# Query products as three fp32r products, the context modulated on GpSimd

## The chip, the cores and the metric

The kernel runs on one core of a Trainium2 chip. The metric is the device time of one execution in microseconds (us), lower is better. Before the change three runs took 1552.02, 1554.79 and 1555.33 us, a median of 1554.79 us.

The five engines of the core each work through their own queue in order: PE (TensorE, the matrix unit; its weight loads are listed as PEld), DVE (VectorE), ACT (ScalarE), POOL (GpSimd) and SP (SyncE, which here only issues DMAs). They wait for one another by semaphores.

## What is computed

The program runs two layers of a transformer with conditioning and a third block with a state-space branch and a mixture of experts, in float32, for 256 tokens and a width of 1024. The change touches only the beginning: the modulated RMS norm of the tokens `x` and of the context `ctx` (256 tokens each), and the query projection of the first attention. Cut to that:

```python
def rmsnorm(x, g):
    y = x * lax.rsqrt(jnp.mean(x * x, axis=-1, keepdims=True) + 1e-6)
    return y * g

def modulate(x, shift, scale):
    return x * (1.0 + scale) + shift

# layer 0: shift and scale are columns of silu(c) @ ada_w + ada_b
h  = modulate(rmsnorm(x,   norm1_g), shift,   scale)      # from c
hc = modulate(rmsnorm(ctx, norm1_g), shift_c, scale_c)    # from c_ctx
q, k, v = jnp.split(h @ wqkv, 3, axis=-1)
qc, kc, vc = jnp.split(hc @ wqkv, 3, axis=-1)
# only k and v are needed of the context
```

## The kernel before

Tokens lie along the free axis and the 1024 features along eight groups of 128 partitions, so `x[:, n]` and `cx[n]` are tiles of 128 by 256. The program is one long list of instructions per engine, in the order in which the Python code calls them; no scheduler moves anything.

**Precision.** Most products take three fast fp32r matmuls (`mm3`): a weight tile `w` is cut into a high part `wh` (ScalarE copy, line 146) and a low part `wl` (VectorE subtraction, line 134), the activations into `hH` and `hL`, and the product is wh·hH + wh·hL + wl·hH. `Stream.split_to(u)` cuts weight units up to u; a unit is 128 by 1024, eight 128 by 128 tiles. Weights come in megabyte DMAs (two units) through a ring of four buffers `st`.

**The query stage** is the loop `for n in ks` over the eight groups n of input features. It alone uses plain fp32 matmuls: `Stream.raw()` hands out the uncut weight unit of group n, and line 625 multiplies its eight tiles with `full`, the modulated `x` of group n. The sums of all eight output tiles stay in four PSUM buffers `ps_q` until the end of the loop.

Shift and scale of group n come up in the same loop. `products(n)` multiplies a megabyte of conditioning weights (line 512, in the middle of tile n-2), ScalarE copies the result to `pa_s` (line 515), `columns(n)` turns it into four columns of `raw` by small matmuls (line 523, at the end of tile n-2). `finish_x(n)` then makes shift and scale of `x` on VectorE (lines 492 and 493), `modulate` multiplies `x` by the scale and the row of reciprocal norms (`na`, line 529, VectorE), and ScalarE adds the shift twice, into `full` (line 532) and `hH` (line 533); VectorE makes `hL` (line 534). This is done for group n+1 after two of the eight products of group n.

**The context** needs the sums of its squares (`sums(cx)`, end of tile 0), its reciprocal norms (`row_rstd(1, ...)`, end of tile 2), and then the same modulation: `modulate_c` does up to two groups at the end of each tile from n = 3 on, with shift and scale on ScalarE (lines 498 and 499), the multiplication on VectorE and the split on both. GpSimd does nothing in this stage.

**The key stage** follows at once: eight tiles of 24 fp32r products each, which read `hH` and `hL` of `x` and the context side by side, 512 columns wide, so it needs all sixteen groups modulated, and weight unit 8 cut (`split_to(n + 3)` in the last two tiles).

Of the kernel before, what the change touches and what calls it, by code (L numbers as in the profile page):

```python
# [8 lines left out]
F32 = mybir.dt.float32  # L9
# [3 lines left out]
AF = mybir.ActivationFunctionType  # L13
ALU = mybir.AluOpType
# [3 lines left out]
P = 128  # L18
T = 256
D = 1024  # L20
KD = 8
# [86 lines left out]
class Stream:  # L108
# [51 lines left out]
    def more(self, n, defer=False):  # L160

        self.fill(self.pos // 8 // 2 + self.ring)
        self.split_to(self.pos // 8 + n, defer)

    def raw(self):

        u = self.pos // 8
        w = self.slots[u // 2][:, u % 2].rearrange("p (a c) -> p a c", a=8)
        if u % 2:
            del self.slots[u // 2]  # L170
        self.pos += 8
        self.nu = max(self.nu, u + 1)
        return w

    def take(self, n, ahead=None):

# [248 lines left out]
def build(ctx, tc, ap):  # L425
    b = Builder(ctx, tc, ap)
    nc = tc.nc
    ctx.enter_context(tc.manual_schedule())
    cp = ctx.enter_context(tc.tile_pool(name="const", bufs=1))
# [8 lines left out]
    x = cp.tile([P, KD, T], F32, name="x")  # L438
# [31 lines left out]
    ks = range(KD)  # L470
# [19 lines left out]
    def finish_x(n):  # L490

        nc.vector.tensor_scalar(AB[n][:, 0, 0:1], raw[:, n, 0:1], b.vecs[:, ab + n:ab + n + 1], None, op0=ALU.add)
        nc.vector.tensor_scalar(AB[n][:, 1, 0:1], raw[:, n, 2:3], b.vecs[:, n1 + n:n1 + n + 1], bsc[:, n:n + 1],
                                op0=ALU.mult, op1=ALU.add)

    def finish_c(n):

        nc.scalar.activation(AB[n][:, 0, 1:2], raw[:, n, 1:2], AF.Identity, bias=b.vecs[:, ab + n:ab + n + 1])
        nc.scalar.activation(AB[n][:, 1, 1:2], raw[:, n, 3:4], AF.Identity, bias=bsc[:, n:n + 1],
                             scale=b.vecs[:, n1 + n:n1 + n + 1])  # L500

    parts_ = {}

# [13 lines left out]
    def columns(n):  # L517

        if n >= KD:
            return  # L520
        p_ = parts_.pop(n)
        for j in range(2):
            nc.tensor.matmul(raw[:, n, 2 * j:2 * j + 2], lhsT=p_[:, j * P:(j + 1) * P], rhs=b.cst("sel"), start=False, stop=True,
                             skip_group_check=True)

    def modulate(src, rows, n, i, full=None):

        t = b.wk.tile([P, T], F32, tag="na", name="na", bufs=3)
        nc.vector.scalar_tensor_tensor(t, src[n], AB[n][:, 1, i:i + 1], rows, op0=ALU.mult, op1=ALU.mult)
        yield  # L530
        if full is not None:
            nc.scalar.activation(full, t, AF.Identity, bias=AB[n][:, 0, i:i + 1])
        nc.scalar.activation(hH[:, n, 1 - i], t, AF.Identity, bias=AB[n][:, 0, i:i + 1])
        nc.vector.scalar_tensor_tensor(hL[:, n, 1 - i], t, AB[n][:, 0, i:i + 1], hH[:, n, 1 - i], op0=ALU.add, op1=ALU.subtract)
        yield

    for n in ks:
        AB[n] = cp.tile([P, 2, 2], F32, name=f"ab{n}")
    nc.scalar.activation(bsc[:, :2], b.ones2, AF.Silu)
    st.limit = 0  # L540
    for i in range(2):
# [50 lines left out]
    columns(1)  # L592
    rows_x, rows_c = rps[:, :T], rps[:, T:]
    psq = [b.ps.tile([P, 2, T], F32, tag="ps", name="ps_q") for _ in range(4)]
    ready, fulls = [], {}

    def modulate_x(n):
        finish_x(n)
        fulls[n] = b.wk.tile([P, T], F32, tag="rp_b", name="full", bufs=2)
        for _ in modulate(xs, rows_x, n, 0, fulls[n]):  # L600
            pass

    def modulate_c():
        todo = []
        for i in ready[:2]:
            finish_c(i)
            todo.append(modulate(cx, rows_c, i, 1))
            next(todo[-1])
        del ready[:2]
        for o in todo:  # L610
            next(o)

    modulate_x(0)
    for n in ks:
        w = st.raw()
        for i in range(KD):
            if i == 2 and n + 1 < KD:
                modulate_x(n + 1)
            if i == 2 and n == 2:
                total(1, accs_c)  # L620
            if i == 5 and n == 2:
                r4 = rstd_of(1)
            if i == 4:
                products(n + 2)
            nc.tensor.matmul(psq[i // 2][:, i % 2], lhsT=w[:, i], rhs=fulls[n], start=(n == 0 and i % 2 == 0), stop=(n == KD - 1),
                             skip_group_check=True)
        columns(n + 2)
        if n == 0:
            accs_c = sums(cx)
        if n == 2:  # L630
            row_rstd(1, r4)
        ready.append(n)
        if n >= 3:
            modulate_c()
        if n in (1, 3, 4, 5, 6):
            load_w()
        if n == 3:
            nc.scalar.dma_start(crow[:, 0], ap["c"].to_broadcast([P, D]))
            nc.scalar.dma_start(crow[:, 1], ap["c_2"].to_broadcast([P, D]))
        if n == 4:  # L640
            for t_, o in ((b.csts, "csts"), (b.vecs, "vecs")):
                c0 = CHEAD if o == "csts" else VHEAD
                nc.scalar.dma_start(t_[:, c0:], ap[o][:, c0:])
        if n >= KD - 2:
            st.nu = max(st.nu, KD)
            st.split_to(n + 3)
    while ready:
        modulate_c()
    st.limit = st.n
    nc.scalar.activation(qT[:, 0:2], psq[0], AF.Copy, scale=0.125)  # L650
    st.more(2)
# [1662 lines left out]
```

## Time and profile before

| | |
|---|---|
| median of 3 runs | 1554.79 us |
| the profiled execution | 1555.31 us |
| its span in the profile | 1553.5 us |
| PE busy | 1483.4 us, 95% of the span |
| DVE, ACT, POOL busy | 986.0, 669.0 and 274.2 us |
| mean granted TensorE clock | 0.989 |

Times within the profile count from the start of the span. The query stage runs from 20.9 to 62.5 us, the key stage from 62.1 to about 107 us. A timeline row gives the start, the duration, the engine, the line and what is written from what; durations include the time an instruction takes to drain, so that neighbours of one engine overlap a little. One fp32 matmul leaves two records, one fp32r matmul one.

### The profile page before, as it was taken

How to read it: one execution, taken by the hardware profiler on the slowest of the kernel's cores; microseconds unless marked ns; L12 is line 12 of the kernel's file. 1: busy time of each engine (PE TensorE's matmuls, PEld its weight loads, DVE VectorE, ACT ScalarE, POOL GpSimd, SP SyncE). 2: the span in 40 equal slices, each digit the busy share in tenths (PEclk: the TensorE clock that was granted, in tenths of full speed). 3: DMA queues.
4: the chain of work that ended last, by engine and by line, in shares of the span. 5: the costliest groups of instructions: out<-in, count | busy, mean ns of one | idle time of the engine just before them, and what ended most of it. 6: DMA issues, size and time to landing. Idle time of an engine off the chain costs nothing. (4 is left out here: it accounts for less than half of the span.)

```text
span 1553.5 us, 28280 instructions
## 1 busy us (share of the span) xinstructions
PE 1483.4 (95%) x11184; PEld 1189.5 (77%) x11184; DVE 986.0 (63%) x1850; ACT 669.0 (43%) x1175; POOL 274.2 (18%) x439
## 2 busy tenths in 40 slices
PE   6999898999999899999899999999999999999996
PEld 4789588999999899999899998999634444444332
DVE  3698858887888788796988867565423333323332
ACT  3523645444454454453677765343322222222222
POOL 0070560000100100021067668001100000000000
PEclk9999999999999899998999999999999999999999
DMA  9678215987956479786354554677489999999995
GB/s 375 232 244 273 94 69 210 340 333 283 355 201 235 172 263 350 290 325 241 126 176 162 178 176 145 218 277 301 188 303 412 420 420 420 421 420 420 421 420 215
DMA packets 71429, 431.93 MB, mean 278 GB/s; under 512 B 8176, under 2 KB 8688, under 8 KB 28416
## 3 DMA queue, kind: packets, MB, share of 16 engines
q1 hardware_dynamic: 68656, 422.77, 70.9%
q0 software_dynamic: 1344, 4.80, 0.9%
q10 hardware_dynamic: 1296, 2.55, 0.5%
q8 instruction: 88, 1.44, 0.4%
q14 instruction: 45, 0.37, 0.1%
HBM read 429.01 MB, written 1.08 MB: 277 GB/s over the span
## 5 line engine op out<-in xcount | busy, mean ns | idle before, releaser
L134 DVE TENSOR_TENSOR wl<-st,wh 128x1024 fp32r<-128x1024 f32 x294 | 365.0, 1250 | 70.4 <-ACT wh L146 70.1
L146 ACT ACTIVATE wh<-st 128x1024 fp32r<-128x1024 f32 x294 | 306.2, 1055 | 109.7 <-PE ps_r L281 41.9
L280 PE MATMUL ps_f<-hh,wh 128*128 128x256 f32 x672 | 189.2, 282 | 1.7 <-ACT hh L380 1.3
L282 PE MATMUL ps_f<-hh,wl 128*128 128x256 f32 x672 | 189.1, 281 | 0.7 <-DVE wl L134 0.7
L281 PE MATMUL ps_f<-hl,wh 128*128 128x256 f32 x672 | 189.0, 281 | 0.1
L395 DVE SCALAR_TENSOR_TENSOR ada<-ada,crow 128x1024 f32<-128x1024 f32 x128 | 164.5, 1293 | 20.4 <-DMA ada<-in_ada 20.4
L340 POOL TENSOR_TENSOR sq<-sq 128x256 f32<-128x256 f32 x30 | 38.9, 1303 | 577.8 <-ACT sq L338 577.4
L280 PEld LDWEIGHTS ps_f<-hh,wh 128*128 128x128 f32 x672 | 127.2, 189 | 2.2 <-ACT hh L380 1.5
L282 PEld LDWEIGHTS ps_f<-hh,wl 128*128 128x128 f32 x672 | 127.1, 189 | 1.0 <-DVE wl L134 1.0
L281 PEld LDWEIGHTS ps_f<-hl,wh 128*128 128x128 f32 x672 | 127.1, 189 | 0.4 <-DVE hl L383 0.4
L280 PE MATMUL ps_ssd<-hh,wh 128*128 128x256 f32 x352 | 101.4, 288 | 0.0
L281 PE MATMUL ps_r<-gL,wh 128*128 128x256 f32 x352 | 98.7, 280 | 0.0
L280 PE MATMUL ps_r<-gH,wh 128*128 128x256 f32 x352 | 98.7, 280 | 0.0
L282 PE MATMUL ps_r<-gH,wl 128*128 128x256 f32 x352 | 98.7, 280 | 0.0
L282 PE MATMUL ps_ssd<-hh,wl 128*128 128x256 f32 x352 | 98.6, 280 | 0.0
L281 PE MATMUL ps_ssd<-hl,wh 128*128 128x256 f32 x352 | 98.6, 280 | 0.0
L1818 DVE TENSOR_SCALAR xb<-gtp,A,mod 128x256 f32<-128x256 f32 (+2 forms) x52 | 27.3, 526 | 111.3 <-ACT xb L1816 111.2
L1816 ACT ACTIVATE xb<-gtp,mod,A 128x256 f32<-128x256 f32 (+2 forms) x52 | 28.5, 549 | 118.5 <-PE gtp L1836 118.4
L1806 POOL TENSOR_TENSOR WG<-G,pwq 128x256 f32<-128x256 f32 (+2 forms) x24 | 14.1, 607 | 363.5 <-DVE G L1802 363.5
L1836 PEld LDWEIGHTS gtp<-G,utH 128*128 128x128 f32 x208 | 39.2, 188 | 45.9 <-DVE xb L1818 19.7
L274 ACT ACTIVATE oH<-wr 128x512 fp32r<-128x512 f32 (+2 forms) x53 | 33.4, 630 | 92.9 <-DVE wr L2094 80.3
L280 PEld LDWEIGHTS ps_ssd<-hh,wh 128*128 128x128 f32 x352 | 66.3, 188 | 1.0 <-issue 1.0
(616 smaller groups left out, 4167.7 us busy)
## 6 DMA issues: line engine op xcount, KB each, us to landing
st<-in_ws SPq DMA_DIRECT2D x151, 1024.0 KB, 6.5
ada<-in_ada SPq DMA_DIRECT2D x128, 512.0 KB, 5.0
w<-in_we SPq DMA_DIRECT2D x40, 1024.0 KB, 19.8
w_st<-in_we SPq DMA_DIRECT2D x40, 1024.0 KB, 19.8
w_y<-in_we SPq DMA_DIRECT2D x32, 1024.0 KB, 19.8
w_ut<-in_we SPq DMA_DIRECT2D x30, 1024.0 KB, 19.8
w_h<-in_we SPq DMA_DIRECT2D x21, 1024.0 KB, 19.8
x<-in_we SPq DMA_DIRECT2D x10, 1024.0 KB, 19.8
```

The lines of the kernel that those rows point to most:

```text
L134: self.b.nc.vector.tensor_tensor(lo.rearrange("p a c -> p (a c)"), w, h.rearrange("p a c -> p (a c)"), op=ALU.subtract)
L146: nc.scalar.activation(h.rearrange("p a c -> p (a c)"), w, AF.Copy)
L274: self.nc.scalar.activation(h, src, AF.Copy)
L280: nc.tensor.matmul(out, lhsT=h[:, k], rhs=xh, start=start, stop=False, skip_group_check=True)
L281: nc.tensor.matmul(out, lhsT=h[:, k], rhs=xl, start=False, stop=False, skip_group_check=True)
L282: nc.tensor.matmul(out, lhsT=lo[:, k], rhs=xh, start=False, stop=stop, skip_group_check=True)
L340: nc.gpsimd.tensor_tensor(self.acc[tag], self.acc[tag], sq, op=ALU.add)
L395: self.nc.vector.scalar_tensor_tensor(junk, w, 1.0, crow, op0=ALU.mult, op1=ALU.mult, accum_out=dst[:, j:j + 1])
L1806: nc.gpsimd.tensor_tensor(cut(WG, tt), cut(G, tt), ws_[:, tt][:, :, None].to_broadcast([P, n, c]), op=ALU.mult)
L1816: nc.scalar.activation(out[:, k, :n], tp[:, i, :n], AF.Identity, scale=A, bias=B)
L1818: nc.vector.tensor_scalar(out[:, k, :n], tp[:, i, :n], A, B, op0=ALU.mult, op1=ALU.add)
L1836: nc.tensor.matmul(tp[:, i, :n], lhsT=hl_[:, tt, k * P:(k + 1) * P], rhs=G[:, tt, :n], start=(i == 0 and tt == 0 and hl_ is utH), stop=(tt ...
```

## The change

`raw()` goes; the query products become `mm3` with cut weights. `x` of group n+2 is modulated at the end of tile n, ahead of the context, and the fp32 copy `full` is no longer made. Of the context, GpSimd now multiplies all eight groups by the row of reciprocal norms (after tile 2) and then each by its scale; VectorE makes shift and scale for two groups at once (`finish_c`), ScalarE and VectorE only add the shift and split (`out_h`). Line numbers in the changed kernel are lower by some ten to sixteen.

```diff
     def finish_c(n):
-        nc.scalar.activation(AB[n][:, 0, 1:2], raw[:, n, 1:2], AF.Identity, bias=b.vecs[:, ab + n:ab + n + 1])
-        nc.scalar.activation(AB[n][:, 1, 1:2], raw[:, n, 3:4], AF.Identity, bias=bsc[:, n:n + 1],
-                             scale=b.vecs[:, n1 + n:n1 + n + 1])
+        s_ = slice(n, n + 2)
+        nc.vector.tensor_tensor(ABc[:, 0, s_], raw[:, s_, 1], b.vecs[:, ab + n:ab + n + 2], op=ALU.add)
+        nc.vector.tensor_tensor(ABc[:, 1, s_], raw[:, s_, 3], b.vecs[:, n1 + n:n1 + n + 2], op=ALU.mult)
+        nc.vector.tensor_tensor(ABc[:, 1, s_], ABc[:, 1, s_], bsc[:, s_], op=ALU.add)
...
+    def out_h(t, n, i, o):
+        nc.scalar.activation(hH[:, n, 1 - i], t, AF.Identity, bias=o)
+        nc.vector.scalar_tensor_tensor(hL[:, n, 1 - i], t, o, hH[:, n, 1 - i], op0=ALU.add, op1=ALU.subtract)
...
     def modulate_x(n):
+        if n >= KD:
+            return
         finish_x(n)
-        fulls[n] = b.wk.tile([P, T], F32, tag="rp_b", name="full", bufs=2)
-        for _ in modulate(xs, rows_x, n, 0, fulls[n]):
-            pass
+        t = b.wk.tile([P, T], F32, tag="na", name="na", bufs=3)
+        nc.vector.scalar_tensor_tensor(t, x[:, n], AB[n][:, 1, 0:1], rows_x, op0=ALU.mult, op1=ALU.mult)
+        out_h(t, n, 0, AB[n][:, 0, 0:1])
+
+    def modulate_c(n):
+        finish_c(n)
+        for i in (n, n + 1):
+            nc.gpsimd.tensor_scalar(cx[i], cx[i], ABc[:, 1, i:i + 1], None, op0=ALU.mult)
+        for i in (n, n + 1):
+            out_h(cx[i], i, 1, ABc[:, 0, i:i + 1])

+    st.split_to(1)
     modulate_x(0)
+    modulate_x(1)
     for n in ks:
-        w = st.raw()
+        w = st.take(KD, 0)
         for i in range(KD):
             if i == 2 and n + 1 < KD:
-                modulate_x(n + 1)
+                st.split_to(n + 2)
...
             if i == 4:
                 products(n + 2)
-            nc.tensor.matmul(psq[i // 2][:, i % 2], lhsT=w[:, i], rhs=fulls[n], start=(n == 0 and i % 2 == 0), stop=(n == KD - 1),
-                             skip_group_check=True)
+            b.mm3(psq[i // 2][:, i % 2], w[i], hH[:, n, 1], hL[:, n, 1], n == 0 and i % 2 == 0, n == KD - 1)
         columns(n + 2)
+        modulate_x(n + 2)
         if n == 0:
             accs_c = sums(cx)
         if n == 2:
             row_rstd(1, r4)
-        ready.append(n)
-        if n >= 3:
-            modulate_c()
+            rows_cs = b.wk.tile([P, T], F32, tag="rp_b", name="rows_cs", bufs=2)
+            nc.scalar.activation(rows_cs, rows_c, AF.Copy)
+            for k in ks:
+                nc.gpsimd.tensor_tensor(cx[k], cx[k], rows_cs, op=ALU.mult)
+        if 3 <= n < 7:
+            modulate_c(2 * n - 6)
...
         if n >= KD - 2:
-            st.nu = max(st.nu, KD)
             st.split_to(n + 3)
-    while ready:
-        modulate_c()
```

Where instructions stand now is shown at three places. First ScalarE from the context's first split on, that is from the end of tile 3 to tile 5; `hH<-na` is a group of `x`, with its number behind `ab`, `hH<-cx` a group of the context, `wh` a weight unit, `pa_s` the copy that `columns` waits for. Before:

```order
L498 ACTIVATE ab_114<-ms,vecs 128x1 [waits DMAHW3_49,PE_49]
L499 ACTIVATE ab_114<-ms,bsc,vecs 128x1
L498 ACTIVATE ab_115<-ms,vecs 128x1
L499 ACTIVATE ab_115<-ms,bsc,vecs 128x1
L533 ACTIVATE hH<-na,ab_114 128x256 [waits DVE_49]
L533 ACTIVATE hH<-na,ab_115 128x256 [waits DVE_49]
L638 DMA crow<-in_c 128x1024 [waits DMAHW3_49]
L639 DMA crow<-in_c 128x1024 [waits DMAHW4_49]
L532 ACTIVATE full<-na,ab_119 128x256 [waits DVE_49]
L533 ACTIVATE hH<-na,ab_119 128x256
L515 ACTIVATE pa_s<-pa 128x256 [waits PE_49]
```

And in the changed kernel:

```order
L518 ACTIVATE hH<-na,ab_119 128x256 [waits DVE_49]
L518 ACTIVATE hH<-cx,abc 128x256 [waits Pool_49] x2
L625 DMA crow<-in_c 128x1024 [waits DMAHW5_49]
L626 DMA crow<-in_c 128x1024 [waits DMAHW6_49]
L146 ACTIVATE wh<-st 128x1024
L506 ACTIVATE pa_s<-pa 128x256 [waits PE_49,Activation_49]
L518 ACTIVATE hH<-na,ab_120 128x256 [waits DVE_49]
```

Two activations of the context that wait for GpSimd now stand ahead of a weight split and of `pa_s` in each round.

Second GpSimd's whole part of the stage, which begins with the row that loads its code and has no counterpart before:

```order
L619 ISA
L619 TENSOR_TENSOR cx<-cx,rows_cs 128x256 [waits DMAHW1_49,Activation_49]
L619 TENSOR_TENSOR cx<-cx,rows_cs 128x256 x3
L619 TENSOR_TENSOR cx<-cx,rows_cs 128x256 [waits DMAHW2_49]
L619 TENSOR_TENSOR cx<-cx,rows_cs 128x256 x3
L591 TENSOR_SCALAR cx<-cx,abc 128x256 [waits DVE_49,Pool_49]
L591 TENSOR_SCALAR cx<-cx,abc 128x256 [waits Pool_49]
```

All eight multiplications by the row stand ahead of the first scaling.

Third VectorE over the same stretch as the first piece, in the changed kernel:

```order
L585 SCALAR_TENSOR_TENSOR na<-x,ab_119,rows 128x256 [waits DVE_49]
L519 SCALAR_TENSOR_TENSOR hL<-na,ab_119,hH 128x256 [waits Activation_49]
L489 TENSOR_TENSOR abc<-ms,vecs 128x2
L490 TENSOR_TENSOR abc<-ms,vecs 128x2
L491 TENSOR_TENSOR abc<-abc,bsc 128x2 [waits DVE_49]
L519 SCALAR_TENSOR_TENSOR hL<-cx,abc,hH 128x256 [waits Activation_49] x2
L134 TENSOR_TENSOR wl<-st,wh 128x1024 [waits Activation_49]
L482 TENSOR_SCALAR ab_120<-ms,vecs 128x1 [waits PE_49]
L483 TENSOR_SCALAR ab_120<-ms,vecs,bsc 128x1
L585 SCALAR_TENSOR_TENSOR na<-x,ab_120,rows 128x256 [waits DVE_49]
```

The context's three small instructions stand behind `hL` of `x`, and the low part of a weight unit ahead of the next group's shift and scale.

## Rows read from the trace of the kernel before

**Rows 1.** Stretches: length; busy PE, PEld, DVE, ACT, POOL (count); clock; DMA share; GB/s.
```profile
30.00:62.00 32.00, 31.61 (x211) 24.36 (x204) 15.65 (x51) 14.66 (x41) 0.00 (x0) 1.00 0.72 264
62.00:107.00 45.00, 45.00 (x194) 36.08 (x193) 41.18 (x78) 18.34 (x31) 23.36 (x15) 1.00 0.70 240
...
1165.00:1553.50 388.50, 368.34 (x2502) 156.06 (x2494) 123.93 (x234) 86.74 (x193) 11.63 (x20) 0.99 0.96 399
```
**Rows 2.** Timeline of PE from the end of tile 3 into tile 4.
```profile
43.89 0.50 PE L523 MATMUL ms<-csts,pa_s 128*128 128x2 f32 x4
...
46.15 1.07 PE L512 MATMUL pa<-v,qT 128*32 128x256 f32 x16
47.15 1.99 PE L625 MATMUL ps_q<-full,st 128*128 128x256 f32 x8
49.00 0.61 PE L523 MATMUL ms<-csts,pa_s 128*128 128x2 f32 x4
```
**Rows 3.** Timeline of PE in the value stage: first and last of 59 consecutive fp32r products.
```profile
107.49 0.28 PE L764 MATMUL ps_v<-wh,hL 128*128 128x256 f32 x1
...
114.26 0.28 PE L762 MATMUL ps_v<-wh,hH 128*128 128x256 f32 x1
```
**Rows 4.** Timeline of all engines where the key stage begins.
```profile
60.48 1.04 ACT L146 ACTIVATE wh<-st 128x1024 fp32r<-128x1024 f32 x1
61.55 1.22 DVE L134 TENSOR_TENSOR wl<-st,wh 128x1024 fp32r<-128x1024 f32 x1 [0.46 <-ACT wh L146]
...
62.83 0.50 PE L282 MATMUL ps_k<-hH,wl 128*128 128x512 f32 x1
```
**Rows 5.** Timeline of all engines up to the end of tile 2.
```profile
17.64 0.38 ACT L515 ACTIVATE pa_s<-pa 128x256 f32<-128x256 f32 x1 [4.51 <-PE pa L512]
...
19.41 0.22 DVE L492 TENSOR_SCALAR ab<-ms,vecs 128x1 f32<-128x1 f32 x1 [2.06 <-PE ms L523]
...
20.92 3.57 PE L625 MATMUL ps_q<-full,st 128*128 128x256 f32 x8 [1.55 <-ACT full L532]
...
25.42 1.99 PE L625 MATMUL ps_q<-full,st 128*128 128x256 f32 x8
...
27.10 2.53 ACT L564 ACTIVATE sq<-cx 128x256 f32<-128x256 f32 x5 [0.19 <-DVE acc L566]
...
32.35 0.50 PE L523 MATMUL ms<-csts,pa_s 128*128 128x2 f32 x4
...
38.70 0.69 PE L583 MATMUL rows<-csts,rs_r 128*128 128x128 f32 x4
```
**Rows 6.** Groups of POOL instructions over the whole span: count, busy us, mean ns, idle before.
```profile
L1806 POOL TENSOR_TENSOR WG<-G,ppf 128x256 f32<-128x256 f32 x2 | 1.2, 612 | 0.1
...
L831 POOL TENSOR_SCALAR od<-csts,orr 128x128 f32<-128x128 f32 x16 | 9.7, 618 | 0.8
...
L304 POOL TENSOR_SCALAR rs_u<-rs_t 128x2 f32<-128x2 f32 x24 | 6.1, 256 | 2.1
```
**Rows 7.** Timeline of POOL: rotation of the first query tile, and of the last.
```profile
76.55 1.62 POOL L681 TENSOR_TENSOR qT<-qT,csts 128x256 f32<-128x256 f32 x1
...
121.01 0.63 POOL L681 TENSOR_TENSOR qT<-qT,csts 128x256 f32<-128x256 f32 x1
```
**Rows 8.** Timeline of all engines in tile 5, up to its end.
```profile
52.48 0.48 DVE L529 SCALAR_TENSOR_TENSOR na<-x,ab,rows 128x256 f32<-128x256 f32 x1
52.99 0.51 ACT L532 ACTIVATE full<-na,ab 128x256 f32<-128x256 f32 x1 [1.39 <-DVE na L529]
53.41 0.49 ACT L533 ACTIVATE hH<-na,ab 128x256 fp32r<-128x256 f32 x1
53.81 0.36 ACT L515 ACTIVATE pa_s<-pa 128x256 f32<-128x256 f32 x1
53.93 0.48 DVE L534 SCALAR_TENSOR_TENSOR hL<-na,ab,hH 128x256 fp32r<-128x256 f32 x1 [0.97 <-ACT hH L533]
54.22 0.61 PE L523 MATMUL ms<-csts,pa_s 128*128 128x2 f32 x4
```

More of the change, by code (lines that the diff above doesn't have):

```diff
@@ L163, in more @@
         self.split_to(self.pos // 8 + n, defer)
[L165 to L173, printed above, removed]
     def take(self, n, ahead=None):
@@ L524, in columns @@
                              skip_group_check=True)
[L526 to L535, printed above, removed]
+    def out_h(t, n, i, o):
+        nc.scalar.activation(hH[:, n, 1 - i], t, AF.Identity, bias=o)
+        nc.vector.scalar_tensor_tensor(hL[:, n, 1 - i], t, o, hH[:, n, 1 - i], op0=ALU.add, op1=ALU.subtract)
     for n in ks:
-        AB[n] = cp.tile([P, 2, 2], F32, name=f"ab{n}")
+        AB[n] = cp.tile([P, 2, 1], F32, name=f"ab{n}")
+    ABc = cp.tile([P, 2, KD], F32, name="abc")
     nc.scalar.activation(bsc[:, :2], b.ones2, AF.Silu)
@@ L594, in build @@
     psq = [b.ps.tile([P, 2, T], F32, tag="ps", name="ps_q") for _ in range(4)]
-    ready, fulls = [], {}
     def modulate_x(n):
+        if n >= KD:
+            return
         finish_x(n)
-        fulls[n] = b.wk.tile([P, T], F32, tag="rp_b", name="full", bufs=2)
-        for _ in modulate(xs, rows_x, n, 0, fulls[n]):
-            pass
[L603 to L611, printed above, removed]
+        t = b.wk.tile([P, T], F32, tag="na", name="na", bufs=3)
[8 more added lines that the diff above has]
+    st.split_to(1)
     modulate_x(0)
+    modulate_x(1)
     for n in ks:
-        w = st.raw()
+        w = st.take(KD, 0)
         for i in range(KD):
             if i == 2 and n + 1 < KD:
-                modulate_x(n + 1)
+                st.split_to(n + 2)
             if i == 2 and n == 2:
```

## The prediction

> **What bounds the kernel now.** I read the stretches first. In the query stage PE is busy for 31.6 of 32 us and in the key stage for 45.0 of 45, while DVE and ACT are about half busy in the query stage and GpSimd not at all [rows 1]. The reader is to see that PE sets the end there, so that a shorter PE list helps only while the other engines keep up, and that the key stage has no slack to swallow a late start. The last 388 us move 399 GB/s with the DMA engines 96% busy [rows 1]; those loads go into buffers that earlier stages give back, so a late start moves them too. I take it that the stages behind shift one for one.
>
> Next the timeline of PE gives the price of one tile: between the ends of two `columns`, 44.39 and 49.61, it takes 5.2 us, of which the eight fp32 products take two times about 1.9, the conditioning products 1.0 and `columns` 0.5 [rows 2]. Then the timelines of ACT and DVE give the steps of the chain by which one group's columns lead to the next, and the groups of POOL the price of its work; both come below.
>
> **What PE gains.** An fp32r product of this shape starts 0.117 us behind the one before: 59 of them between 107.49 and 114.26, so 6.77 by 58 [rows 3]. 24 of them are 2.8 us against 3.8 for eight fp32 ones. So a tile could take 4.3 us in place of 5.2, a gain of 1.0 for each of eight tiles, if PE still set the pace.
>
> **The first four tiles: level.** ACT and DVE each get a weight split per tile, 1.04 for `wh` and 1.22 for `wl` [rows 4]. They lose on ACT the eight `full` and the sixteen small context activations, and on DVE the eight multiplications of the context, so neither is full at 4.3 us; what decides is where the work stands. The first `wl` (`wh` from 18.0, behind `pa_s` of group 1, `wl` to 20.3) stands ahead of `finish_x(0)`, which now starts at 19.41, so the first product comes at 21.8 in place of 20.92 [rows 5]. The first tile begins at the lower clock level (four products in 3.57, the next four in 1.99, that is 1.2 and 2.4 GHz) and will do so again [rows 5]. At the end of tile 0 ACT makes `hH` of group 2, eight squares of the context (five of them 2.53 [rows 5]) until about 32.2, then `wh` of unit 2, and only then `pa_s` of group 3, for which `columns` at the end of tile 1 waits: it ends near 34.1, before 32.85 [rows 5]. The context's norms follow at 40.2 (before 39.39 [rows 5]), and tile 3, which runs at PE's new pace, closes at 44.4. Before it closed at 44.39 [rows 2]. The gain of four tiles has paid for the splits in front.
>
> **GpSimd's price.** Two inputs of 128x256 take 0.61 to 0.63 us when DVE is quiet and 1.62 beside DVE's long instructions with two inputs from SBUF [rows 6, 7]. During the eight multiplications DVE has one `wl` and one `hL` of that kind, 1.7 us; at two and a half times the price that costs 1.0 more, so eight take 5.3 + 1.0 = 6.3. Bounds: 5.0 and 13.0. A scaling by a column is nearest to line 831, the same instruction at 128 columns: 0.618 [rows 6]. Line 304 at 2 columns takes 0.256 [rows 6], about 0.22 undisturbed, so 0.40 for 126 columns, and 256 would cost 1.02. Bounds: 0.62, as much as two inputs of that length, and 1.3 if DVE gets in its way. I take 1.02, since line 831 is the same operation.
>
> **The wait that takes the gain.** ACT's queue is in order, and from the end of tile 3 on two activations of the context, which wait for GpSimd, stand ahead of the weight split and of `pa_s`. Behind them wait PE (`columns`, and the next unit's products) and DVE (`wl`).
> First round: the rows' copy is made by 41.4; GpSimd multiplies until 47.9 and scales two groups until 49.9; ACT splits the second (0.46 behind), cuts unit 5 (0.95 until the next can start), copies `pa_s` (0.35), PE does `columns` (0.55). That ends at 52.2, before at 49.61 [rows 2]: 2.6 late.
> Every further round, from `columns` to `columns`: 1.05 until `na` is done (the `finish_x` pair, then 0.48 [rows 8]) and 0.35 in which DVE still makes `wl`; `hH` 0.55, `hL` 0.40; three small DVE instructions 0.5; GpSimd 0.1 + 2.04; second `hH` of the context 0.46; `wh` 0.95; `pa_s` 0.36; `columns` 0.55. Sum 7.3, before 5.2. So tile 5 closes at 59.5; before at 54.83 [rows 8]: 4.7 late.
> The tail: the same steps up to `wh` of unit 7 (6.5, at 66.0), its `wl` (1.2), the last two groups (0.5 + 2.1 + 0.5), `wh` of unit 8 (1.05) and its `wl` (1.25). The third key product, which waits for that `wl`, starts at 72.5; before at 62.83 [rows 4]. **9.7 late.** In tiles 6 and 7 PE has only 2.8 us of work each, all covered.
>
> Costs at nothing: DMAs keep their number. `st` buffers come free after the cut instead of after PE's reads, so weights load no later. The four loads issued by ACT stand behind the waiting activations, some 4 to 7 us later, and are first read in the key stage. The idle stretches on PE may bring back the lower clock; within the tiles the chain covers it, at the start of the key stage it could cost up to 1.8, half of the 3.57 that the slow products took [rows 5]. I put 0 into the sum and keep 1.8 for the range.
>
> **Sum.** The profiled execution took 1555.3 us, 0.5 above the median of the three runs. 1555.3 + 9.7 = **1565.0**, that is +0.6%. A measurement of this kernel can tell some 0.2%, or 3.1 us, from no change.
>
> **Rivals.**
> *Cheap scalings.* With 0.62 for one, four pairs on the chain save 0.8 each: +6.5, 1561.8. For it: two inputs of this length cost no more. Against it: line 831. *Cheaper still.* Two inputs cost 0.612 for 256 columns, some 0.39 above the 0.22 of line 304 [rows 6]; if one input cost half of that, a scaling would take 0.42, four pairs would save 1.2 each: +4.9, 1560.2. The Trainium skill, "GPSIMD Engine Reference", section 3 (Performance versus the Vector engine), speaks for this: it puts a short one-input loop at 1.03 cycles an element and one with two inputs at about 2.6, at 1.2 GHz an estimated 0.22 us for 256. By that rule 128 columns would take some 0.3 in all, and the trace has 0.618, so the two do not agree for this instruction.
> *GpSimd disturbed throughout.* With 1.62 for each multiplication the first round ends 6.7 later: +16.4, 1571.7. Against it: DVE stands still in that stretch, waiting for ACT.
> *Absorbed.* If some later stage waited for a load that is not moved, the end would stay: 1555.3. The full key stage speaks against it [rows 1].
> *Faster: ACT is not held.* If context and x overlap so that the round is shorter than PE's 4.3 us, tiles 4 and 5 end at 53.0 and tiles 6 and 7 at 58.6, and the third key product comes at 59.1, 3.7 earlier: 1551.6. This needs a round of 7.3 to shrink by 3.0. Without GpSimd's 2.04, less the 0.41 by which the context's two `hH` then follow each other, it still is 5.7, and the tail 9.9, which gives +2.7, 1558.0. So it decides only if 1.4 us more of steps read here as serial overlap.
>
> **How the numbers follow.** Scalings at 1.02: 0.45; at 0.62: 0.15; at 0.42: 0.10; disturbed: 0.12; absorbed: 0.08; faster: 0.10. The range runs from 1558.0, GpSimd costing nothing, to 1572, the disturbed case, which also holds the forecast with the clock's 1.8 and with scalings of 1.3; it leaves out the last two cases, 0.18. Slower is the first four, 0.82, same 0.08, faster 0.10.
>
> **What would show it.** In the timeline of ACT, waits for GpSimd ahead of the context's `hH`, the first from about 46 to 50; in that of PE, `columns` ending near 44.4, 52.2 and 59.5 and PE idle before each of the last two; query products 0.117 apart; line 591 near 1.0 and line 619 near 0.8 us on POOL; the third key product near 72.5. I am wrong if PE stays busy from tile 3 on, or if the key stage starts late and the end does not move.

## The result and the profile after

The changed kernel takes 1567.43 us, the median of four runs (1564.42 to 1572.82); the kernel before, run beside it, takes 1553.40 us (four runs, 1548.96 to 1555.33). The ratio is 1.0093, 95% interval 1.0067 to 1.0119. A second series later in the study gave 1.0088 (1.0061 to 1.0115). The change makes the kernel slower by some 14 us. That lies in the range and on the forecast side; 9.7 us had been forecast (9.7 by 1555.31 is 0.62%), which is below the first interval and only just inside the second.

| | before | after |
|---|---|---|
| the profiled execution | 1555.31 us | 1565.84 us |
| its span | 1553.5 us | 1564.0 us |
| third key product | 62.83 us | 76.90 us |
| first value product | 107.26 us | 121.34 us |
| POOL busy | 274.2 us | 291.0 us |
| mean granted TensorE clock | 0.989 | 0.986 |

The profiled execution after lies in the shorter half of its runs and that of before in the longer, so the spans differ by 10.5 where the medians differ by 14.0. The value stage starts 14.1 us late (121.34 against 107.26), which is as much as the medians differ by.

First the stretches, which answer to [rows 1] (columns as there). The key stage now ends near 121, so the second and third line split the old key stage:

```profile
30.00:62.00 32.00, 25.48 (x213) 19.62 (x212) 17.72 (x49) 12.91 (x26) 10.43 (x12) 0.89 0.64 247
62.00:77.00 15.00, 10.12 (x64) 8.88 (x62) 8.13 (x19) 7.31 (x13) 3.65 (x4) 0.89 0.42 146
77.00:107.00 30.00, 30.00 (x129) 24.13 (x130) 27.55 (x52) 13.33 (x23) 14.68 (x10) 1.00 0.64 225
1165.00:1564.00 399.00, 378.43 (x2567) 160.49 (x2566) 128.26 (x241) 89.42 (x199) 12.88 (x22) 0.99 0.97 398
```

PE, busy for 31.6 of 32 us before, now has 6.5 us of gaps there, and 4.9 more up to 77. GpSimd has 14 us of new work. The key stage itself is as full as before, it only starts later, and the last stretch moves 398 GB/s, where it moved 399.

The timeline of PE in the changed kernel, at the points that answer to [rows 2, 4, 5, 8] (`ms` of line 514 is `columns`, `pa` of line 503 `products`, `rows` the context's reciprocal norms, line 272 the third product of a weight tile):

```profile
21.56 0.58 PE L270 MATMUL ps_q<-hH,wh 128*128 128x256 f32 x1 [2.28 <-ACT hH L518]
...
24.72 1.94 PE L503 MATMUL pa<-v,qT 128*32 128x256 f32 x16
...
28.36 0.50 PE L514 MATMUL ms<-csts,pa_s 128*128 128x2 f32 x4
...
35.27 0.61 PE L514 MATMUL ms<-csts,pa_s 128*128 128x2 f32 x4 [2.29 <-ACT pa_s L506]
...
39.40 1.75 PE L503 MATMUL pa<-kT,qT 128*32 128x256 f32 x16
...
44.12 0.71 PE L568 MATMUL rows<-csts,rs_r 128*128 128x128 f32 x4 [1.01 <-DVE na L585]
...
48.67 0.50 PE L514 MATMUL ms<-csts,pa_s 128*128 128x2 f32 x4
...
56.43 0.61 PE L514 MATMUL ms<-csts,pa_s 128*128 128x2 f32 x4 [3.14 <-ACT pa_s L506]
...
63.87 0.61 PE L514 MATMUL ms<-csts,pa_s 128*128 128x2 f32 x4 [0.87 <-ACT pa_s L506]
...
76.90 0.50 PE L272 MATMUL ps_k<-hH,wl 128*128 128x512 f32 x1 [0.36 <-DVE wl L134]
```

Three times `columns` waits for `pa_s`, and each time the row ends in ACT. The timeline of ACT says why:

```profile
31.47 2.54 ACT L549 ACTIVATE sq<-cx 128x256 f32<-128x256 f32 x5 [0.18 <-DVE acc L551]
33.91 1.04 ACT L146 ACTIVATE wh<-st 128x1024 fp32r<-128x1024 f32 x1
34.86 0.36 ACT L506 ACTIVATE pa_s<-pa 128x256 f32<-128x256 f32 x1
...
53.26 0.51 ACT L518 ACTIVATE hH<-cx,abc 128x256 fp32r<-128x256 f32 x1 [2.58 <-POOL cx L591]
54.18 0.51 ACT L518 ACTIVATE hH<-cx,abc 128x256 fp32r<-128x256 f32 x1 [0.41 <-POOL cx L591]
...
55.05 1.06 ACT L146 ACTIVATE wh<-st 128x1024 fp32r<-128x1024 f32 x1 [0.36 <-issue]
56.02 0.36 ACT L506 ACTIVATE pa_s<-pa 128x256 f32<-128x256 f32 x1
...
60.72 0.51 ACT L518 ACTIVATE hH<-cx,abc 128x256 fp32r<-128x256 f32 x1 [1.98 <-POOL cx L591]
```

From 50.7 to 54.7 ACT serves nothing but the context, standing for 3.0 of these 4.0 us, while a weight split and `pa_s`, on which PE waits, stand behind it. At 33.9 the same happens with the context's squares in place of GpSimd: they and a split stand ahead of `pa_s`.

GpSimd's instructions, which answer to [rows 6], from the groups of POOL and then from its timeline:

```profile
L591 POOL TENSOR_SCALAR cx<-cx,abc 128x256 f32<-128x256 f32 x8 | 7.3, 925 | 14.7 <-DVE abc L491 14.7
L619 POOL TENSOR_TENSOR cx<-cx,rows_cs 128x256 f32<-128x256 f32 x8 | 6.8, 880 | 44.9 <-ACT rows_cs L617 44.9
```

```profile
45.33 6.75 POOL L619 TENSOR_TENSOR cx<-cx,rows_cs 128x256 f32<-128x256 f32 x8 [44.88 <-ACT rows_cs L617]
52.29 1.86 POOL L591 TENSOR_SCALAR cx<-cx,abc 128x256 f32<-128x256 f32 x2 [0.21 <-DVE abc L491]
```

The `ISA` row at the head of GpSimd's list leaves no row in the timeline, and the first multiplication starts 0.07 us after the copy `rows_cs` ends (45.26). What that instruction does, no run here shows; it costs nothing that can be seen.

### The profile page after: what moved, and what is told of

The parts are those of the page before. It is cut to its first block, busy times and chain, and to the rows that moved or that the text cites. A ratio compares the mean times of both kernels' runs of the same rounds, so it can differ in the third digit from the quotient of the medians.

```text
span 1564.0 us, 28418 instructions
## 1 busy us (share of the span) xinstructions
PE 1485.3 (95%) x11248; PEld 1193.6 (76%) x11248; DVE 997.4 (64%) x1862; ACT 671.0 (43%) x1160; POOL 291.0 (19%) x455
## 3 DMA queue, kind: packets, MB, share of 16 engines
HBM read 429.01 MB, written 1.08 MB: 275 GB/s over the span
## 5 line engine op out<-in xcount | busy, mean ns | idle before, releaser
L134 DVE TENSOR_TENSOR wl<-st,wh 128x1024 fp32r<-128x1024 f32 x302 | 376.3, 1254 | 79.7 <-ACT wh L146 79.5
L146 ACT ACTIVATE wh<-st 128x1024 fp32r<-128x1024 f32 x302 | 314.5, 1055 | 112.0 <-PE ps_r L271 48.1
L1790 POOL TENSOR_TENSOR WG<-G,pwq 128x256 f32<-128x256 f32 (+2 forms) x24 | 14.1, 608 | 362.7 <-DVE G L1786 362.7
L264 ACT ACTIVATE oH<-wr 128x512 fp32r<-128x512 f32 (+2 forms) x53 | 33.4, 630 | 92.8 <-DVE wr L2078 80.2
```

The costliest lines, as they stand in the source:

```text
L134: self.b.nc.vector.tensor_tensor(lo.rearrange("p a c -> p (a c)"), w, h.rearrange("p a c -> p (a c)"), op=ALU.subtract)
L146: nc.scalar.activation(h.rearrange("p a c -> p (a c)"), w, AF.Copy)
L264: self.nc.scalar.activation(h, src, AF.Copy)
L1790: nc.gpsimd.tensor_tensor(cut(WG, tt), cut(G, tt), ws_[:, tt][:, :, None].to_broadcast([P, n, c]), op=ALU.mult)
```

## The experiments

Four theories of where the time goes. **A**: the order of ACT's queue; the context's two splits wait for GpSimd ahead of `wh` and `pa_s`, so each round runs through one long chain. **B**: the waits on ACT only cover another loss, on PE itself (its lower clock after each gap) or the like, so that taking them away changes little. **C**: the slowness of GpSimd's instructions, not their place. **D**: a separate loss before all that, the context's squares ahead of `pa_s` at the end of tile 1. The measure in all of them is the start of the third key product, 62.83 before and 76.90 after.

### The context's split one tile later

GpSimd scales two groups as in the changed kernel; ACT and DVE split them only at the end of the next tile, behind `x`:

```diff
-    def modulate_c(n):
+    def scale_c(n):
         finish_c(n)
         for i in (n, n + 1):
             nc.gpsimd.tensor_scalar(cx[i], cx[i], ABc[:, 1, i:i + 1], None, op0=ALU.mult)
+
+    def split_c(n):
         for i in (n, n + 1):
             out_h(cx[i], i, 1, ABc[:, 0, i:i + 1])
...
+        if 4 <= n:
+            split_c(2 * n - 8)
         if 3 <= n < 7:
-            modulate_c(2 * n - 6)
+            scale_c(2 * n - 6)
```

> The changed kernel, with the context's two hH and hL of a round issued one tile later than their scalings on GpSimd, so that ScalarE cuts the next weight unit and copies pa_s before it meets them. Same instructions, other order. In the changed kernel the columns of tiles 3, 4 and 5 end at 49.2, 57.0 and 64.5 us and the third key product starts at 76.9. Theory A (ScalarE's queue is held by two activations that wait for GpSimd): the two rounds shrink from 7.9 and 7.4 to about 4.5 to 5, the third key product starts at 65 to 68, some 10 us earlier, and the total falls by 8 to 12 us. Rival B (the weight splits and the lower clock are what costs, GpSimd's wait only stands where another would): the rounds stay above 6.5 and the third key product comes after 74.

> The lag of one tile alone, timed in several rounds. If the 6.2 us by which the third key product is late in its profile (69.03 against 62.83) go through to the end, the ratio to the kernel before is 1.0040, between 1.002 and 1.006. If later stages give a late start back, it is below 1.002; if they add to it, above 1.006.

The timeline of PE with the split one tile later (the last two `columns` and the third key product; the one before them starts at 50.33):

```profile
54.78 0.50 PE L514 MATMUL ms<-csts,pa_s 128*128 128x2 f32 x4
...
59.24 0.50 PE L514 MATMUL ms<-csts,pa_s 128*128 128x2 f32 x4
...
69.03 0.50 PE L272 MATMUL ps_k<-hH,wl 128*128 128x512 f32 x1 [0.52 <-DVE wl L134]
```

The rounds take 4.45 and 4.46 us in place of 7.87 and 7.44, which is PE's own pace, and `columns` waits for nothing. The key stage starts 7.9 us earlier, though this kernel's first four tiles are even 1.7 us later (50.33 against 48.67). That is A; B is out. A start of 65 to 68 had been expected under A, and it is 69.03: behind tile 3 the gain is 9.5 us, of which the later first tiles take 1.7 back. Some waiting stays behind the last tile, where nothing is left to put in front:

```profile
65.36 0.51 ACT L518 ACTIVATE hH<-cx,abc 128x256 fp32r<-128x256 f32 x1 [2.08 <-POOL cx L591]
```

One execution took 1561.38 us. Timed in a series, the kernel takes 1558.12 us (12 runs), 1.0011 times the kernel before (0.9997 to 1.0025; 1555.59 us, 29 runs), which can't be told from no change. The third key product repeats (68.95), but the end is some 4.5 us earlier than that start would let one expect, and the expectation of 1.0040 failed; more on this below.

### The context multiplied on VectorE, in the same place

```diff
+        ts_ = []
         for i in (n, n + 1):
-            nc.gpsimd.tensor_scalar(cx[i], cx[i], ABc[:, 1, i:i + 1], None, op0=ALU.mult)
+            ts_.append(b.wk.tile([P, T], F32, tag="na", name="na", bufs=3))
+            nc.vector.scalar_tensor_tensor(ts_[-1], cx[i], ABc[:, 1, i:i + 1], rows_c, op0=ALU.mult, op1=ALU.mult)
         for i in (n, n + 1):
-            out_h(cx[i], i, 1, ABc[:, 0, i:i + 1])
+            out_h(ts_[i - n], i, 1, ABc[:, 0, i:i + 1])
...
-            for k in ks:
-                nc.gpsimd.tensor_tensor(cx[k], cx[k], rows_cs, op=ALU.mult)
```

> The changed kernel with the context multiplied on VectorE again (one instruction for norm and scale), in the same place of the queues; GpSimd does nothing in this stage. Theory A: the place in the queue remains, only the wait is shorter: the first round loses the wait for the eight multiplications (7.9 to about 6.3), every later one some 1.1 us; the third key product near 72, 5 us earlier than in the changed kernel and 9 later than before. Rival C (GpSimd as such is the cost, by its speed or by disturbing VectorE): the rounds fall to PE's 4.3 to 5 and the third key product comes at 65 to 67.

The timeline of PE with the context on VectorE:

```profile
56.24 0.61 PE L514 MATMUL ms<-csts,pa_s 128*128 128x2 f32 x4 [1.45 <-ACT pa_s L506]
...
63.09 0.61 PE L514 MATMUL ms<-csts,pa_s 128*128 128x2 f32 x4 [0.41 <-ACT pa_s L506]
...
74.66 0.40 PE L272 MATMUL ps_k<-hH,wl 128*128 128x512 f32 x1
```

Without GpSimd the key stage is only 2.2 us earlier than in the changed kernel, where 5 had been expected, and the waits for `pa_s` are still there; one execution took 1568.31 us. Tile 3 closes 1.5 us later here (its `columns` start at 50.19), so behind it the gain is 3.8. The place in the queue is most of the loss, what VectorE saves over GpSimd in that place a small part. C is out as the main cause.

### The context's squares on GpSimd, ahead of the loop

```diff
+    acc_c = b.wk.tile([P, T], F32, tag="rp_a", name="acc", bufs=2)
+    sq_c = b.wk.tile([P, T], F32, tag="rp_b", name="sqc", bufs=2)
+    nc.gpsimd.tensor_tensor(acc_c, cx[0], cx[0], op=ALU.mult)
+    for k in ks[1:]:
+        nc.gpsimd.tensor_tensor(sq_c, cx[k], cx[k], op=ALU.mult)
+        if k < KD - 1:
+            nc.gpsimd.tensor_tensor(acc_c, acc_c, sq_c, op=ALU.add)
+    accs_c = acc_c, sq_c
...
-        if n == 0:
-            accs_c = sums(cx)
```

> The changed kernel with the squares and sums of the context on GpSimd, from when the context lands, in place of ScalarE and VectorE at the end of tile 0. Theory D for the first three tiles (eight squares on ScalarE stand ahead of the cut of unit 2 and of pa_s of group 3, PE waits for it and falls back to the lower clock in tile 2): no wait of 2.3 us before the columns at the end of tile 1, tile 2 at the higher clock, the norms' rows end near 40 in place of 44.8, the third key product near 72. Rival E (the clock falls in tile 2 whatever ScalarE does, because the first tile is slow): the rows end after 43.5 and the third key product comes after 75.5.

> The context's squares on GpSimd alone, timed in several rounds. If the 9.7 us by which the third key product is late in its profile (72.53 against 62.83) go through, the ratio to the kernel before is 1.0062, between 1.004 and 1.0085, some 0.003 below the changed kernel. If the 4.4 us that the cure saves are lost again on the way, as the one look seemed to say, it is 1.009.

The timeline of PE with the squares on GpSimd, at the points from 35.27 on of the fence above:

```profile
32.88 0.50 PE L514 MATMUL ms<-csts,pa_s 128*128 128x2 f32 x4
...
39.76 0.71 PE L568 MATMUL rows<-csts,rs_r 128*128 128x128 f32 x4 [1.01 <-DVE na L585]
...
44.31 0.50 PE L514 MATMUL ms<-csts,pa_s 128*128 128x2 f32 x4
...
52.07 0.61 PE L514 MATMUL ms<-csts,pa_s 128*128 128x2 f32 x4 [3.15 <-ACT pa_s L506]
...
72.53 0.50 PE L272 MATMUL ps_k<-hH,wl 128*128 128x512 f32 x1 [0.29 <-DVE wl L134]
```

The wait of 2.29 at the end of tile 1 is gone, and tile 3 closes 4.4 us earlier (44.31 against 48.67). All that follows is the changed kernel's, 4.4 us earlier: the wait of 3.15 is the same, and so is the rest up to the key stage. D is a loss of its own, 4.4 us in size between these two profiles. Over all profiles tile 3 closes at 49.17 to 50.83 in the six with the squares on ACT (changed kernel, lag, context on VectorE, doubled scalings) and at 44.81 to 45.46 in the three with them on GpSimd (two of this kernel, one of both cures), so the size is between 3.7 and 6.0. Rival E is out: the granted clock stays at 1.00 in tile 2 (the rows are further below). One execution, 1567.43 us, showed nothing of the gain; the series does: 1562.61 us (12 runs), ratio 1.0042 (1.0026 to 1.0058), while the third key product came at 73.38 in its profile.

### Every scaling twice

```diff
         for i in (n, n + 1):
             nc.gpsimd.tensor_scalar(cx[i], cx[i], ABc[:, 1, i:i + 1], None, op0=ALU.mult)
+            nc.gpsimd.tensor_scalar(cx[i], cx[i], b.ones2[:, 0:1], None, op0=ALU.mult)
```

> The changed kernel with every scaling on GpSimd done twice, the second time by ones. Theory A: each added pair lengthens each of the four places on the chain by about 1.8 us: rounds of 9.7 and 9.3, the third key product near 84, the total up by some 7 us. If GpSimd's scalings lay beside other work (rival B), the third key product stays within 2 us of 76.9.

The timelines of PE and then of POOL with doubled scalings:

```profile
59.21 0.96 PE L514 MATMUL ms<-csts,pa_s 128*128 128x2 f32 x4 [5.17 <-ACT pa_s L506]
...
68.77 0.61 PE L514 MATMUL ms<-csts,pa_s 128*128 128x2 f32 x4 [1.74 <-ACT pa_s L506]
...
85.70 0.50 PE L272 MATMUL ps_k<-hH,wl 128*128 128x512 f32 x1 [0.52 <-DVE wl L134]
```

```profile
53.04 0.94 POOL L591 TENSOR_SCALAR cx<-cx,abc 128x256 f32<-128x256 f32 x1 [0.21 <-DVE abc L491]
...
56.00 0.92 POOL L592 TENSOR_SCALAR cx<-cx,ones 128x256 f32<-128x256 f32 x1
```

A pair with its two more instructions takes 3.9 us (53.04 until the fourth ends at 56.92) in place of 1.86, so four pairs take 8.1 more; tile 3 closes 0.75 later here than in the changed kernel. That makes 8.8, and the key stage is 8.8 us later (7 had been expected); one execution took 1576.43 us. GpSimd's time is on the path in full.

### GpSimd alone, in the kernel before

The fp32 products and all places stay; only the context's multiplications move to GpSimd:

```diff
-        todo = []
-        for i in ready[:2]:
-            finish_c(i)
-            todo.append(modulate(cx, rows_c, i, 1))
-            next(todo[-1])
+        todo = ready[:2]
...
+        for i in todo:
+            finish_c(i)
+            nc.gpsimd.tensor_scalar(cx[i], cx[i], AB[i][:, 1, 1:2], None, op0=ALU.mult)
+        for i in todo:
+            nc.scalar.activation(hH[:, i, 0], cx[i], AF.Identity, bias=AB[i][:, 0, 1:2])
+            nc.vector.scalar_tensor_tensor(hL[:, i, 0], cx[i], AB[i][:, 0, 1:2], hH[:, i, 0], op0=ALU.add, op1=ALU.subtract)
...
+            rows_cs = b.wk.tile([P, T], F32, tag="na", name="rows_cs", bufs=3)
+            nc.scalar.activation(rows_cs, rows_c, AF.Copy)
+            for k in ks:
+                nc.gpsimd.tensor_tensor(cx[k], cx[k], rows_cs, op=ALU.mult)
```

> The kernel before, with its fp32 query products, and only the context's two multiplications moved to GpSimd, in the old places of the queues. Theory A: ScalarE is held here too, and behind its two waiting activations now stand full of the next group of x and pa_s; columns of tile 4 end near 52.8 in place of 49.6, the next round takes about 6.3 in place of 5.2, and the third key product comes at 67 to 70, the total some 5 us up. Rival F (without weight splits on ScalarE and VectorE GpSimd's time lies beside PE's longer fp32 products): the third key product stays within 1.5 us of 62.8.

> The kernel before with the context's multiplications on GpSimd and nothing else, timed in several rounds. Its third key product came at 67.96 against 62.83, 5.1 late: ratio 1.0033, between 1.0015 and 1.005. If GpSimd were hidden behind the slower fp32 products, 1.000.

The timeline of PE of the second of these runs:

```profile
51.13 0.61 PE L523 MATMUL ms<-csts,pa_s 128*128 128x2 f32 x4 [1.45 <-ACT pa_s L515]
...
63.48 3.72 PE L625 MATMUL ps_q<-full,st 128*128 128x256 f32 x16 [1.46 <-ACT full L532]
...
68.11 0.50 PE L282 MATMUL ps_k<-hH,wl 128*128 128x512 f32 x1 [0.44 <-DVE wl L134]
```

Even beside the slower products GpSimd isn't hidden: the key stage starts 5.3 us late. The series gives 1561.11 us (12 runs), ratio 1.0021 (1.0006 to 1.0036), where 1.0033, and 1.0015 at the least, had been expected. The two profiles of this one kernel agree on the start to 0.2 us (67.96 and 68.11), and their executions took 1560.84 and 1567.60: single executions differ by several us behind the key stage, so starts are compared by profiles and ends by series.

### Both cures, and a better version

The lag and the squares on GpSimd together:

> Both cures in the changed kernel: the squares of the context on GpSimd, and the context's hH and hL one tile later than their scalings. If the hold of ScalarE's queue and the squares ahead of pa_s in tile 0 are separate costs, the gains add: 7.9 us of the first and 4.4 of the second off the third key product, which comes near 64.6 (before 62.8, changed 76.9), and the total is within 0.3% of the kernel before, at 1.000 to 1.003 of it. If they are one cost seen twice (a rival: what is gained in the first tiles is waited away in the last), the third key product comes after 67 and the ratio is above 1.004.

The series gives 1554.13 us (10 runs), ratio 0.9992 (0.9973 to 1.0011), and the third key product comes at 64.12. A total of 1.000 to 1.003 and a start of 64.6 had been expected. The loss of the change is undone by the later split and by the squares on another engine, its three parts kept. The better version cuts weight units earlier (unit 0 ahead of the norms, units 7 and 8 a tile sooner) and gives GpSimd the last four scalings at the end of tile 5:

```diff
+    st.split_to(1)
...
-                st.split_to(n + 2)
+                st.split_to(n + 2 if n < 6 else 9)
+            if i == 5 and n == 5:
+                st.split_to(8)
...
-        if 3 <= n < 7:
-            modulate_c(2 * n - 6)
+        if 4 <= n:
+            split_c(2 * n - 8)
+        if 3 <= n < 6:
+            scale_c(2 * n - 6)
+        if n == 5:
+            scale_c(6)
...
-        if n >= KD - 2:
+        if n == KD - 1:
```

> The same two cures, and the weight units cut earlier: unit 0 ahead of the norms of x, unit 7 and 8 one tile sooner, the last scalings of the context at the end of tile 5. What is left then is PE's own list: the first product near 20.9, tiles of about 4.4 us, the third key product at 58.5 to 61, 2 to 4 us ahead of the kernel before, the total at 0.997 to 0.999 of it. If VectorE or ScalarE is full at that pace (a rival: the splits themselves cost what the cheaper products give), the rounds stay above 4.8 and the third key product comes after 62.

The timeline of PE of this version:

```profile
52.84 0.50 PE L514 MATMUL ms<-csts,pa_s 128*128 128x2 f32 x4
...
60.09 0.40 PE L272 MATMUL ps_k<-hH,wl 128*128 128x512 f32 x1
```

No wait is left in front of the last `columns` or the key products, and the key stage starts 2.7 us earlier than before. The series gives 1551.31 us (10 runs), ratio 0.9968 (0.9950 to 0.9986): faster than both kernels.

### Both kernels once more

> The kernel before once more, for a second profile of it. So far every variant ended some 3 us earlier against it than its third key product is late. If its first profile showed an unusually early start, the third key product now comes near 66; if the start repeats as it does in the other kernels, it comes between 62.5 and 63.2, and the 3 us are regained behind it.

> The changed kernel once more, timed in several rounds beside the same runs of the kernel before. Its third key product repeats near 76.9, 14 late. If the late start goes through whole, the ratio is 1.0090; if 3 us are regained as in the other variants, 1.0071. Either is between 1.006 and 1.0105.

The third key product repeats: 62.47 before, 77.74 after. So the first profile of before showed no unusual start. The changed kernel took 1567.70 us (6 runs) against 1555.34 (11 runs), ratio 1.0088 (1.0061 to 1.0115), which lies at the first of its two expectations but leaves the second inside its interval.

Start and end together, the starts against the mean of before's two profiles, 62.65, the ends as the ratio's difference from one times 1555 us:

| kernel | third key product | start, us | end, us (95%) |
|---|---|---|---|
| changed | 76.90, 77.74 | +14.3, +15.1 | +14.5 (10.4 to 18.5), +13.7 (9.5 to 17.9) |
| squares on GpSimd | 72.53, 73.38 | +9.9, +10.7 | +6.5 (4.0 to 9.0) |
| split one tile later | 69.03, 68.95 | +6.4, +6.3 | +1.7 (-0.5 to 3.9) |
| GpSimd alone | 67.96, 68.11 | +5.3, +5.5 | +3.3 (0.9 to 5.6) |
| both cures | 64.12 | +1.5 | -1.2 (-4.2 to 1.7) |
| better version | 60.09 | -2.6 | -5.0 (-7.8 to -2.2) |

From row to row the end follows the start about one for one, but in five of six rows the series ends 2 to 5 us earlier than the start says. The plain differences of the medians give, from the top, 14.0 and 12.4, 7.0, 2.5, 5.5, -2.5 and -5.3 us, so that the row of GpSimd alone has no such gap by them. In the profiles the rest of the execution, from the third key product to the end of the span, takes 1490.7 and 1488.0 us in the kernel before and 1483.6 to 1497.7 in all the others, which is too wide to settle 2 to 5 us. Whether later stages give that back to every variant, or the series of before ran a little long, stays open. It changes the sign of the both-cures row alone; that row and the split one tile later can't be told from no change by their ends.

## Why the prediction was right, and which term was too small

**What bounds the kernel: right.** PE's list was the bound, the other engines did not keep up, and the key stage swallowed nothing. The rival that a later stage absorbs the late start is out.

**What PE gains: right.** Where PE waits for nothing a tile takes 4.34 us (the `rows` end at 44.83, the next `columns` at 49.17); 4.3 had been worked out. In the changed kernel the gain is never seen at the end, since the chain sets the pace from tile 4 on; with the split one tile later it is (4.45 a round).

**The first four tiles: level. This step failed, by 4.8 us.** Tile 3 closes at 49.17 (48.67 and 0.50), where 44.4 had been forecast and 44.39 was before. The first product came at 21.56 as forecast (21.8). Three terms were missing or too small.

- The first tile took 7.3 us (21.56 to 28.86). Its products start 0.21 us apart up to 27 and 0.117 apart from there. They are 0.21 apart again at 38 to 39 us, where the granted clock has fallen (rows below), so 0.21 is read as the lower level (1.2 GHz) and 0.117 as the higher (2.4 GHz). The record of the granted clock itself reads 1.00 in the first tile of this execution; in the second profile of the kernel before it reads 0.50 from 22 to 25 us. `products` at 24.72 took 1.94 where it otherwise takes 1.07; the price had been taken from the 3.57 us of [rows 5]. With that the squares ended at 33.91 in place of 32.2, and `columns` at 35.88 in place of 34.1: 1.8.
- `columns` waited 2.29 for `pa_s`. That wait stood in the forecast (its 34.1); what the sum had put at 0 is the lower clock to which PE fell behind it. From the end of these `columns` to the end of `rows` it is 8.95 us; with the squares on GpSimd, where the gap is missing and the clock stays up, the same stretch is 7.09 (33.38 to 40.47): 1.9, of which 0.2 is a wait for `wl` at 36.26.
- `rows` waits 1.01, which the trace puts down to `na` of group 4, now ahead of it; `na` reads one half of the PSUM tile `rps`, and `rows` writes the other. Before it did not wait [rows 5]. The step had nothing for that, and the wait is the same with the squares on GpSimd: 1.0.

The first two shares are those of one execution. The timeline of PE in the second profile of the changed kernel:

```profile
34.36 0.61 PE L514 MATMUL ms<-csts,pa_s 128*128 128x2 f32 x4 [2.29 <-ACT pa_s L506]
...
44.75 0.71 PE L568 MATMUL rows<-csts,rs_r 128*128 128x128 f32 x4 [1.01 <-DVE na L585]
...
49.31 0.50 PE L514 MATMUL ms<-csts,pa_s 128*128 128x2 f32 x4
```

Here the clock rose sooner in the first tile, and `columns` end at 34.97, only 0.9 behind the forecast. But the stretch to the end of `rows` takes 10.49 in place of 8.95, and tile 3 closes at 49.81, 5.4 late. The gap and the lower clock behind it are then the larger part, 3.4.

The granted clock in these places, from the stretches of the changed kernel (columns as in [rows 1]):

```profile
20.00:25.00 5.00, 3.44 (x16) 2.91 (x20) 3.31 (x10) 1.97 (x3) 0.00 (x0) 1.00 1.00 421
...
38.00:43.00 5.00, 5.00 (x38) 3.69 (x38) 2.80 (x15) 0.92 (x2) 0.00 (x0) 0.72 1.02 424
...
57.00:60.00 3.00, 2.96 (x21) 2.30 (x24) 1.95 (x8) 0.51 (x1) 0.24 (x1) 0.65 0.96 330
...
72.00:77.00 5.00, 4.64 (x25) 4.21 (x25) 2.45 (x5) 3.38 (x6) 1.82 (x2) 0.70 0.82 294
```

And most of tile 2 with the squares on GpSimd, where it starts at 33.4:

```profile
33.00:38.00 5.00, 5.00 (x51) 4.29 (x50) 3.47 (x14) 1.85 (x3) 0.00 (x0) 1.00 0.99 397
```

From 38 to 43 PE is busy for all 5 us in the changed kernel, and slower products are time on the path. From 57 and from 72 the chain on ACT covers them: `columns` at 63.87 and the key product at 76.90 still wait. That the clock is free where such a wait follows was right; behind the gap in front of tile 2 no such wait follows, and there it costs time.

**GpSimd's price: right in sum.** The eight multiplications took 6.75 us (6.3 forecast) and a scaling 0.92 (1.02). Forecast for eight and eight: 14.5; measured: 14.1. The two cheap prices among the rivals, 0.62 and 0.42 for a scaling, are out: the trace has 0.925, and the row at 128 columns [rows 6] was the better guide. The rule of the Trainium skill that was weighed there ("GPSIMD Engine Reference", section 3, Performance versus the Vector engine) gives an estimated 0.22 us for the elements of a short one-input loop of that length; the trace does not agree for this instruction. Nor was GpSimd disturbed throughout (1.62 each): its multiplications took 0.88 on average.

**The wait that takes the gain: right.** The first round took 7.87 us (7.8 forecast), the second 7.44 (7.3), the tail 12.42 (13.0). Lag and doubled scalings show that these waits are the cause. A round without GpSimd's time had been put at 5.7; with the context on VectorE it is 6.2 and 6.9, since VectorE's multiplications take some of that time themselves and PE ran at the lower clock in part.

**The sum.** The key stage was late by 14.1 us, not 9.7: the 4.8 of the failed step, less 0.4 over the rounds and the tail. The time forecast, 1565.0, lies closer to the median of 1567.43 than the terms do, because the sum started from an execution of 1555.31, which is 1.9 above the median of before in the comparison; that is luck, and no term of the working is better for it.

**The costs put at nothing.** The loads issued by ACT left 8.3 and 10.5 us later (54.19 against 45.88, 61.62 against 51.10), not 4 to 7. It still cost nothing there: PE is busy for all of 77 to 107.

**The faster rival.** It asked for a round that overlaps the context with `x`. The changed kernel has no such overlap; the split one tile later makes it, and then PE's pace rules the rounds as that rival said.

## What to carry to other kernels

An instruction that waits for a slow engine holds all that stands behind it in its engine's queue, so a short product list is worth nothing until the instructions that feed the bottleneck stand ahead of those that wait; here moving the consumer by one tile gave back 7.9 us, and giving its producer's work to a faster engine 2.2. Before a queue is called level, follow each buffer copy that the bottleneck needs and add up what stands ahead of it, also where the edit did not touch that work. Price a gap on PE with what runs slower behind it, unless another wait covers that too.

## What the runs showed that was not expected

- A scaling of 128x256 by a column took 0.92 us on GpSimd, where the product of two tiles of that size takes 0.612 [rows 6]: the operation with less to read is the dearer one.
- GpSimd and DVE slow each other in either direction. While GpSimd multiplied, a weight split of DVE in the changed kernel took 1.61 where it takes 1.22 [rows 4]; with the split one tile later it kept 1.23, and the pair of scalings that began 0.16 us behind it took 2.80 in place of 1.86. The Trainium skill, "SBUF — State Buffer" (Who interferes with whom), states that a VectorE instruction with two inputs from SBUF contends with a GpSimd instruction that reads SBUF; both traces agree. The timeline of DVE of the changed kernel, and those of DVE and POOL with the split one tile later:

```profile
46.23 1.61 DVE L134 TENSOR_TENSOR wl<-st,wh 128x1024 fp32r<-128x1024 f32 x1 [1.11 <-ACT wh L146]
```

```profile
53.79 1.23 DVE L134 TENSOR_TENSOR wl<-st,wh 128x1024 fp32r<-128x1024 f32 x1
```

```profile
53.95 2.80 POOL L591 TENSOR_SCALAR cx<-cx,abc 128x256 f32<-128x256 f32 x2 [0.21 <-DVE abc L491]
```

- The moment at which PE's clock rose in the first tile differed between executions of the same instructions: `products` at 24.7 took 1.94 us in the first profile of the changed kernel and 1.21 in the second, and with doubled scalings, whose instructions are the same up to there, 1.08 at 25.09.
